# Second half of layer 0's last output projection, token-major, with the key/value stage re-cut by inner tiles

## The chip, the cores and the metric

The kernel runs on one core of a Trainium2 chip. The metric is device time in microseconds (us) for one execution, and the time of the kernel before is the median of three runs. A core has five engines that each run their own instructions strictly in the order in which they are issued: TensorE (PE in the profile; its weight loads are shown as PEld), VectorE (DVE), ScalarE (ACT), GpSimd (POOL) and SyncE (SP), which here issues nearly all DMAs. They wait for one another by semaphores.

## The reference, cut to what matters

A decoder trunk on 256 tokens of 1024 features, in float32. Layer 0 is FFN, short convolution, FFN; then one shared key/value projection is made from its output; layer 1 is FFN, sparse attention on that key/value, FFN. Around the change stand the second FFN of layer 0 and the projection `kv`:

```python
def rmsnorm(x, g):
    y = x * lax.rsqrt(jnp.mean(x * x, axis=-1, keepdims=True) + EPS)
    return y * g

def swiglu_ffn(x, w_in, w_out):              # w_in 1024 x 5632, w_out 2816 x 1024
    gate, up = jnp.split(x @ w_in, 2, axis=-1)
    return (jax.nn.silu(gate) * up) @ w_out

h = h + 0.5 * swiglu_ffn(rmsnorm(h, g), w_in, w_out)     # layer 0's second FFN
kv = (rmsnorm(h, kv_norm) @ w_kv)                        # w_kv 1024 x 1536
kv = kv.reshape(bsz, s, N_BRANCH, 2, N_KV_GROUPS, HEAD_DIM)
```

Branch 0 of `kv` (512 of its 1536 columns) goes on into a compression; branches 1 and 2 (the other 1024 columns: K of both, then V of both) are used as keys and values.

## The kernel before, in words

**Arithmetic.** Each float32 product is made of three matmuls. A weight is split into a high part `wh` and a low part `wl`, an activation into halves that lie side by side in one 128x512 tile (high for 256 tokens, low for 256 tokens), and high x high, low x high and high x low are summed in PSUM.

**Weights.** All weights come through one stream `W` in the order of their use. A chunk of 2048 columns (1 MB) is loaded by SyncE into one of three buffers `ws` (L139). Each chunk holds two units of 1024 columns; of each, ScalarE casts the high part (`wh`, L166) and VectorE subtracts to get the low part (`wl`, L183). There are six buffers of each. `take()` hands out the next unit; `done()` gives its buffer back and calls `pump()`, which issues the conversion of as many further units as have a free buffer. So where `done()` stands in the code is also where the next conversions stand in the queues of ScalarE and VectorE; and with the last unit of a chunk the load of the chunk two further on is issued to SyncE's queue. Nothing overtakes.

**The output projection** (`out_proj`, L471). The hidden activations are 22 tiles of 128 features (`act`). For the two FFN layers that end in it, the first 512 output features are made token-major: for each of the 22 tiles, six matmuls of 512 columns with the activation as the stationary operand (L492 to L494), 132 in all, into one pair of PSUM banks (`mm`). Two VectorE transposes of 32x32 blocks (L500) bring the result out; it goes to DRAM (`back`, two DMAs, L501) and comes back turned, features on the partitions (`come`, two DMAs, L507, into tiles `t`). `joined(m)` then adds two feature tiles to `h` (L513), makes the high halves of the two norms that follow (ScalarE, L294), the squares for the norm (ScalarE L309, summed on GpSimd L311), and the low halves (VectorE, L298). The last 512 features are made feature-major, in four tiles `c` = 4 to 7: for each, 22 matmuls of 512 columns (L532, the high weights) and 22 of 256 columns (L538, the low weights), then two adds from PSUM (L455) and the same norm steps. `joined(0)` and `joined(1)` are issued among these.

**The key/value stage.** Its inputs are `xkv[0..7]`, the normed tiles of `h`: 0 to 3 lie in `kt`, 4 to 7 in tiles `t`. K for all tokens runs over the eight `k`, 48 matmuls of 512 columns (L861 to L863), then V the same; then the four tiles of the compressed branch, eight matmuls of 512 (L351) and eight of 256 columns (L356) each. The sum of squares (`nm.halves()` on GpSimd, L317 and L318; `nm.rows()` on TensorE) becomes the factor `R` (ScalarE L329, VectorE L331), by which the results are scaled afterwards, not the inputs. So TensorE needs `xkv[k]` only when it gets to `k`, and `R` only for the outputs. After it comes the first FFN of layer 1 (L432 to L434).

Of the kernel before, what the change touches and what calls it, by code (L numbers as in the profile page):

```python
# [9 lines left out]
F32 = mybir.dt.float32  # L10
# [6 lines left out]
P = 128  # L17
# [51 lines left out]
def trunk(ctx, tc, A, out):  # L69
# [27 lines left out]
    def bank(shape=(P, 512)):  # L97
        return mk(shape, "a", 4, pool=ps)
# [186 lines left out]
    class Norm:  # L285
# [31 lines left out]
            po.tensor_copy(out=self.q[:, :T], in_=self.sq)  # L317
            po.tensor_tensor(out=self.q[:, T:], in0=self.sq, in1=self.q[:, :T].bitcast(F32), op=ALU.subtract)  # L318

        def rows(self):  # L320

            pb = bank()
            if self.q is None:
                pe.matmul(pb[:, :T], ones, self.sq, start=True, stop=True)
            else:
                for x in range(2):
                    pe.matmul(pb[:, :T], ones.bitcast(F32R), self.q[:, x * T:(x + 1) * T], start=(x == 0), stop=(x == 1))
            s = t1()
            ac.activation(s, pb[:, :T], AF.Sqrt, scale=1.0 / D, bias=epst)  # L329
            r = mk([P, T], "R", 2)  # L330
            ve.reciprocal(r, s)  # L331
            return r
# [135 lines left out]
        if c == ND - 1:  # L468
            norm.low(c)

    def out_proj(lhs, factor, norm, rest=None, cut=(7, 7, 7, 2)):  # L471

        n, i, u = len(lhs), 0, None
        if rest is None:
            head = [(bank(), W.take()[0]) for _ in range(4)]
            a_pass([(o, u, lhs, range(n)) for (o, u), n in zip(head, cut)])
            for c in range(4):
                o, u = head[c]
                a_pass([(o, u, lhs, range(cut[c], 8))])
                W.done(1, False)  # L480
                out_evac(o, c, factor, norm, True)
        else:
            n, o = NF, bank2()
            for k in range(NF):
                if k % 2 == 0:
                    u, = W.take()
                if k == 12:
                    rest()
                wh, wl = [u[x][:, (k % 2) * 512:(k % 2 + 1) * 512] for x in range(2)]
                for tt in range(2):  # L490
                    sh, sl = lhs[k][:, tt * P:(tt + 1) * P], lhs[k][:, T + tt * P:T + (tt + 1) * P]
                    pe.matmul(o[:, tt], sh, wh, start=(k == 0), stop=False)  # L492
                    pe.matmul(o[:, tt], sl, wh, start=False, stop=False)  # L493
                    pe.matmul(o[:, tt], sh, wl, start=False, stop=(k == NF - 1))  # L494
                if k % 2 == 1:
                    W.done()
            d = mk([2, 2, P, T], "back", 1, pool=dr)
            for tt in range(2):
                tb = mk([P, 768], "pr", 6)[:, :512]
                ve.transpose(tb, o[:, tt])  # L500
                sy.dma_start(d[:, tt].rearrange("m p n -> p m n"), tb.rearrange("p (m n) -> p m n", m=2))  # L501
            came = []

        def come():
            for m in range(2):
                came.append(t2([P, 2, T]))
                sy.dma_start(came[m].rearrange("p c (b j) -> p c b j", j=32),  # L507
                             d[m].rearrange("t (b i) (x c j) -> (i x) c (t b) j", i=32, c=2, j=32))

        def joined(m):  # L510
            cs = range(2 * m, 2 * m + 2)
            for c in cs:
                ve.scalar_tensor_tensor(out=h[c], in0=came[m][:, c % 2], scalar=factor, in1=h[c], op0=ALU.mult, op1=ALU.add)  # L513
            for c in cs:
                norm.high(c)
            for c in cs:
                norm.squares(c)
                norm.low(c)

        def tile():  # L520
            nonlocal i, u
            if i % 8 == 0:
                u, = W.take()
            q = slice(i % 8 * P, (i % 8 + 1) * P)
            i += 1
            return u[0][:, q], u[1][:, q], i % 8 == 0

        def wide(o, run, ks, last=None):
            for k in ks:
                while len(run) <= k:  # L530
                    run.append(tile())
                pe.matmul(o, run[k][0], lhs[k], start=(k == 0), stop=(k == last))  # L532

        def narrow(o, run, ks, last=None, free=True):
            for k in ks:
                while len(run) <= k:
                    run.append(tile())
                pe.matmul(o[:, :T], run[k][1], lhs[k][:, :T], start=False, stop=(k == last))  # L538
                if run[k][2] and free:
                    W.done(1, k < n - 1)  # L540

        c = 4
        while c < ND:
            o, run = bank(), []
            if n > 8 and c % 2 and c + 1 < ND:
                wide(o, run, range(n))
                o2, run2 = bank(), []
                wide(o2, run2, [0])
                joined(0)
                narrow(o, run, range(n), n - 1)  # L550
                out_evac(o, c, factor, norm)
                joined(1)
                narrow(o2, run2, range(n), free=False)
                wide(o2, run2, range(1, n), n - 1)
                for _ in range(sum(t[2] for t in run2)):
                    W.done(1, False)
                out_evac(o2, c + 1, factor, norm)
                W.pump(2)
                c += 2
                continue  # L560
            wide(o, run, range(n))
            narrow(o, run, range(n), n - 1)
            if n > 8 and c == 4:
                come()
            out_evac(o, c, factor, norm, n == 8)
            c += 1
        W.pump()
# [249 lines left out]
    def load_bias(j):  # L817
        pp, hg = divmod(j, 4)
        b = kt8[:, j, T:].rearrange("p (a n) -> p a n", a=2)
        src = bass.AP(tensor=row_d.tensor, offset=row_d.offset + (8 * pp + hg) * OHW,  # L820
                      ap=[[1, P], [4 * OHW, 2], [1, 256]])
        for a in range(2):
            if a == 0 or j < 4:
                sy.dma_start(b[:, a:] if j > 3 else b[:, a], src[:, a:] if j > 3 else src[:, a])
        bias[j] = b

    def c_bias(j):
# [15 lines left out]
    xk_a = mk([P, 4, 512], "kt", 1, F32R)  # L843
    xkv = [xk_a[:, k] for k in range(4)] + [t2(dt=F32R) for _ in range(4)]
    nm = Norm([(xkv, G_KV), (xs, G_FFN1 + 8)])
    out_proj(hid, 0.5, nm, rest=rest)
    nm.halves()
    del hid

    def b_full(xk, mid=None, shadow=None, o=None):  # L850
# [52 lines left out]

    kv = {}

    def kv_mid():
        kv["R"] = nm.rows()

    def kv_cols(k):

        if k != 1:
            return
        pt = bank2()[:, 0]
        for tt in range(2):
            pe.transpose(pt[:, tt * P:(tt + 1) * P], kv["R"][:, tt * P:(tt + 1) * P], ident)
        kv["rc"] = mk([P, 2], "rc", 2, pool=tiny)
        ve.tensor_copy(out=kv["rc"], in_=pt[:, 0:2 * P:P])
        kv["kns"] = scaled(ok, kv["rc"])

    ok = b_full(xkv, kv_mid)  # L920
    ov = b_full(xkv, None, kv_cols)
    rc, kns, R1 = kv["rc"], kv["kns"], kv["R"]
    for tt in range(2):
        ac.activation(V[tt], ov[tt], AF.Copy, scale=rc[:, tt:tt + 1])
    W.limit = 5

    own, other = [[act([P, 2, T], F32) for _ in range(2)] for _ in range(2)]
    for c in range(4):
        o, (u,) = bank(), W.take()
        a_pass([(o, u, xkv, range(8))])  # L930
        W.done()
        r = t1()
        ac.copy(r, o[:, T:])
        ve.tensor_tensor(out=r, in0=o[:, :T], in1=r, op=ALU.add)
        po.tensor_tensor(out=own[c // 2][:, c % 2], in0=r, in1=R1, op=ALU.mult)

    KT = mk([P, 2, 528], "kt", 1)
    raw = [mk([P, 16, 64], t, NBUF) for t in ("wh", "wl")]
# [508 lines left out]
def _layout(i):  # L1447
# [3 lines left out]
    for n in ("ffn1", "ffn2"):  # L1451
        w = a[n + "_w_in"]
        ins, outs = [], []
        for w, v, turn in zip(w.reshape(2, 1024, -1), a[n + "_w_out"], (0, n == "ffn2")):
            ins.append(w.reshape(8, 128, 2, NF // 2, 256).transpose(1, 3, 0, 2, 4).reshape(128, -1))
            v = v.reshape(-1, 4, 2, 32, 1024).transpose(0, 2, 3, 1, 4).reshape(-1, 1024)
            if turn:
                outs.append(v.reshape(NF, 128, 2, 512).transpose(1, 2, 0, 3).reshape(128, -1))
                continue
            first = v[:, :512].reshape(FF, 2, 2, 32, 4).transpose(0, 1, 4, 2, 3).reshape(NF, 128, 512).transpose(1, 0, 2)  # L1460
            v = v[:, 512:].reshape(NF, 128, 4, 128).transpose(1, 2, 0, 3)
            outs.append(np.concatenate([x.reshape(128, -1) for x in (first, v)], 1))
# [6 lines left out]
    r["conv_w_in"] = np.concatenate([cv, _rows(w[:, :1024])], 1)  # L1469
    r["conv_w_out"] = _rows(a["conv_w_out"][0])  # L1470
    w = a["w_kv"].reshape(8, 128, 3, 2, 256)
    parts = [p.reshape(8, 128, 512).transpose(1, 0, 2).reshape(128, -1) for p in (w[:, :, 1:, 0], w[:, :, 1:, 1])]
    r["w_kv"] = np.concatenate(parts + [_rows(w[:, :, 0].reshape(1024, 512))], 1)
    for n in ("cmp_w1_k", "cmp_w1_v"):
        r[n] = a[n].reshape(2, 16, 64, 128).transpose(0, 2, 1, 3).reshape(128, -1)
    w = a["attn_w_q"][0]
# [45 lines left out]
```

## Time and profile before

| | |
|---|---|
| runs of the kernel before | 949.6, 949.87, 949.9 us (median 949.87) |
| profiled execution, its own time | 949.64 us |
| span of its trace | 947.9 us (1.7 us lie outside it) |
| TensorE busy | 943.6 us, 4610 matmuls, granted clock 1.0 |
| VectorE, ScalarE, GpSimd busy | 653.8, 534.7, 111.8 us |
| read from and written to HBM | 190.80 and 16.29 MB |

How to read it: the profile's page gives busy time by engine, the chain of work that ended last, and the costliest groups of instructions. The timeline lists instructions in order with their start and length; `x22` means that 22 like instructions in a row were put in one row, and a bracket tells how long the engine idled before it and what released it. Matmuls are pipelined: a 512-column matmul is shown as 0.39 us long, while the next begins 0.227 us after it, so starts and not lengths are counted. The table of windows gives each engine's busy time, the granted TensorE clock and the DMA share of a stretch.

### The profile page before, as it was taken

The numbers are of one execution on the slowest core, as the hardware profiler recorded it, in microseconds if no ns is written. First come the engines' busy times: TensorE is split into PE (matmuls) and PEld (weight loads), VectorE is DVE, ScalarE is ACT, GpSimd is POOL, SyncE is SP. The second block draws the span as 40 slices with busy tenths as digits, with TensorE's granted clock in tenths as the row PEclk, the third lists the DMA queues.
The fourth block names the chain that finished last, engine by engine and source line by source line (L and its number), as shares of the span: only waits on it lengthen the run. The fifth ranks groups of instructions, "written<-read, shape, count | busy, mean of one in ns | idle before, by whom it ended". The sixth has DMA issues, their size and how long they took to land.

```text
span 947.9 us, 12791 instructions
## 1 busy us (share of the span) xinstructions
PE 943.6 (100%) x4610; PEld 789.1 (83%) x4610; DVE 653.8 (69%) x1066; ACT 534.7 (56%) x895; POOL 111.8 (12%) x191
## 2 busy tenths in 40 slices
PE   9999999999999999999999999999999999999998
PEld 8888888888888888888888888888877888888887
DVE  8767655778796667747757676856679787767552
ACT  7645543655465545545647775644589765445440
POOL 3000000211020000001121022200238120000000
PEclk9999999999999999999999999999999999999999
DMA  8888786658646998777647877776511248998750
GB/s 319 255 263 253 229 261 209 232 181 262 222 146 227 253 278 266 240 271 222 222 170 220 254 231 254 262 253 209 199 46 39 96 178 250 284 301 252 263 202 22
DMA packets 163966, 208.43 MB, mean 220 GB/s; under 512 B 124302, under 2 KB 140815, under 8 KB 143424
## 3 DMA queue, kind: packets, MB, share of 16 engines
q1 hardware_dynamic: 163758, 207.37, 67.2%
q8 instruction: 36, 0.59, 0.2%
q10 hardware_dynamic: 144, 0.26, 0.1%
q14 instruction: 28, 0.21, 0.1%
HBM read 190.80 MB, written 16.29 MB: 218 GB/s over the span
## 4 chain that ended last, share of the span: by engine, by line
PE 98%; DVE 1%; ACT 0%; issue 0%
PE mm L434 16%; PE mm L432 16%; PE mm L433 16%; PE a L532 7%; PE a L538 4%; PE mm L493 3%; PE mm L494 3%; PE mm L492 3%; PE a L351 3%; PE mm L655 2%; PE a L591 2%; PE a L590 2%; PE a L589 2%; PE a L356 2%; PE mm L723 2%; PE mm L725 2%
## 5 line engine op out<-in xcount | busy, mean ns | idle before, releaser
L183 DVE TENSOR_TENSOR wl<-ws,wh 128x1024 fp32r<-128x1024 f32 x316 | 387.0, 1245 | 214.0 <-ACT wh L166 205.3
L166 ACT CAST wh<-ws 128x1024 fp32r<-128x1024 f32 x316 | 326.4, 1051 | 230.1 <-DMA ws<-in_ffn_w_in_dram 98.1
L432 PE MATMUL mm<-wh,xs 128*128 128x512 f32 x656 | 255.9, 390 | 0.0
L434 PE MATMUL mm<-wl,xs 128*128 128x512 f32 x656 | 255.4, 389 | 0.0
L433 PE MATMUL mm<-wh,xs 128*128 128x512 f32 x656 | 255.3, 389 | 0.0
L434 PEld LDWEIGHTS mm<-wl,xs 128*128 128x128 f32 x656 | 123.1, 188 | 25.9 <-DVE wl L183 0.5
L433 PEld LDWEIGHTS mm<-wh,xs 128*128 128x128 f32 x656 | 123.2, 188 | 25.4
L432 PEld LDWEIGHTS mm<-wh,xs 128*128 128x128 f32 x656 | 123.2, 188 | 25.3
L311 POOL TENSOR_TENSOR sq<-sq,t 128x256 f32<-128x256 f32 x42 | 35.5, 846 | 385.9 <-ACT t L309 385.2
L390 ACT ACTIVATE t<-mm,rc 128x256 f32<-128x256 f32 x86 | 40.7, 474 | 59.1 <-DVE t L391 44.9
L532 PE MATMUL a<-act,wh 128*128 128x512 f32 x296 | 69.5, 390 | 0.0
L532 PEld LDWEIGHTS a<-act,wh 128*128 128x128 f32 x296 | 54.9, 188 | 11.0
L391 DVE SCALAR_TENSOR_TENSOR t<-mm,rc,t 128x256 f32<-128x256 f32 x86 | 41.5, 482 | 18.4 <-ACT t L390 15.1
L492 PE MATMUL mm<-wh,act 128*128 128x512 f32 x132 | 51.3, 389 | 0.0
L493 PE MATMUL mm<-wh,act 128*128 128x512 f32 x132 | 51.3, 389 | 0.0
L494 PE MATMUL mm<-wl,act 128*128 128x512 f32 x132 | 51.3, 389 | 0.0
L294 ACT ACTIVATE xs<-base 128x256 fp32r<-128x256 f32 x48 | 24.1, 507 | 44.9 <-DVE base L455 31.2
L359 ACT CAST act<-t 128x256 fp32r<-128x256 f32 x96 | 34.6, 405 | 13.0 <-DVE t L801 9.1
L392 DVE STREAM_TRANSPOSE t<-t 128x256 f32<-128x256 f32 x88 | 39.2, 446 | 3.1
L538 PEld LDWEIGHTS a<-act,wl 128*128 128x128 f32 x296 | 37.2, 191 | 1.0
L538 PE MATMUL a<-act,wl 128*128 128x256 f32 x296 | 37.5, 283 | 0.0
L360 DVE TENSOR_TENSOR act<-t,act 128x256 fp32r<-128x256 f32 x96 | 36.9, 423 | 0.5 <-ACT act L359 0.5
(278 smaller groups left out, 1196.5 us busy)
## 6 DMA issues: line engine op xcount, KB each, us to landing
ws<-in_ffn_w_in_dram SPq DMA_DIRECT2D x84, 1024.0 KB, 5.7
ws<-in_ffn_w_out_dram SPq DMA_DIRECT2D x44, 1024.0 KB, 5.6
turn<-t SPq DMA_DIRECT2D x48, 256.0 KB, 2.3
t<-turn SPq DMA_DIRECT2D x48, 256.0 KB, 7.0
ws<-in_conv_w_in_dram SPq DMA_DIRECT2D x12, 1024.0 KB, 5.1
ws<-in_w_kv_dram SPq DMA_DIRECT2D x6, 1024.0 KB, 5.2
ws<-in_conv_w_out_dram SPq DMA_DIRECT2D x4, 1024.0 KB, 5.4
ws<-in_attn_w_q_dram SPq DMA_DIRECT2D x4, 1024.0 KB, 5.5
```

Of the source, the lines that this page charges most:

```text
L166: ac.copy(h, src)
L183: ve.tensor_tensor(out=l, in0=src, in1=h.bitcast(F32), op=ALU.subtract)
L390: ac.activation(s, o[tt][:, :T], AF.Silu, scale=rc[:, tt:tt + 1])
L391: ve.scalar_tensor_tensor(out=s, in0=o[tt][:, T:], scalar=rc[:, tt:tt + 1], in1=s, op0=ALU.mult, op1=ALU.mult)
L432: pe.matmul(o[tt], sh, wh, start=(k == 0), stop=False)
L433: pe.matmul(o[tt], sl, wh, start=False, stop=False)
L434: pe.matmul(o[tt], sh, wl, start=False, stop=(k == 7))
L492: pe.matmul(o[:, tt], sh, wh, start=(k == 0), stop=False)
L493: pe.matmul(o[:, tt], sl, wh, start=False, stop=False)
L494: pe.matmul(o[:, tt], sh, wl, start=False, stop=(k == NF - 1))
L532: pe.matmul(o, run[k][0], lhs[k], start=(k == 0), stop=(k == last))
L538: pe.matmul(o[:, :T], run[k][1], lhs[k][:, :T], start=False, stop=(k == last))
```

## The change

For layer 0's second FFN alone, all 1024 features of the output projection are made token-major, in two halves of 132 matmuls each (`half`, called twice; the tile code above is not run there). The first half's result is fetched (`come`) at `k` = 6 of the second, and joined at `k` = 12 and 15. The second half's result goes to DRAM and comes back right after it, into buffers of `act`. It is joined (features 512 to 1023, which are `xkv[4..7]`) inside the key/value stage, by the `joined` that `out_proj` now returns.

The key/value stage is cut by inner tiles: `kv_full(k)` does K and V of one `k` (12 matmuls of 512 columns, one unit of weights). `kv_full(0..3)` come first, then `k` 0 to 3 of the compressed tiles `c0` and `c1`, then `joined(2)`, `kv_full(4)`, `joined(3)`, `kv_full(5)`, `k` 4 to 7 of `c0` and `c1`, the norm's rows, `kv_full(6)`, `kv_full(7)`, and tiles `c2`, `c3`. The weights lie in DRAM in that order: chunks [k0, k1], [k2, k3], [c0, c1], [k4, k5], [k6, k7], [c2, c3].

In all output projections with a token-major half, the last `done()` no longer pumps; `pump()` follows the half's transposes. `load_bias` issues one DMA where it issued two for four of its eight calls.

```diff
+        def half(step):
+            nonlocal u
+            o = bank2()
+            for k in range(NF):
+                if k % 2 == 0:
+                    u, = W.take()
+                step(k)
...
+                if k % 2 == 1:
+                    W.done(1, k < NF - 1)
+            d = mk([2, 2, P, T], "back", 1, pool=dr)
+            for tt in range(2):
+                tb = mk([P, 768], "pr", 6)[:, :512]
+                ve.transpose(tb, o[:, tt])
+                sy.dma_start(d[:, tt].rearrange("m p n -> p m n"), tb.rearrange("p (m n) -> p m n", m=2))
+            return d
...
+            n, d = NF, half(lambda k: rest() if k == 12 else None)
+            W.pump()
...
+        if whole:
+            d = half(lambda k: come() if k == 6 else joined(k // 3 - 4) if k in (12, 15) else None)
+            come(act)
+            W.pump()
+            return joined
...
-        for a in range(2):
-            if a == 0 or j < 4:
-                sy.dma_start(b[:, a:] if j > 3 else b[:, a], src[:, a:] if j > 3 else src[:, a])
+        for a in range(2):
+            if a == 0:
+                sy.dma_start(b, src)
...
-    out_proj(hid, 0.5, nm, rest=rest)
-    nm.halves()
+    joined = out_proj(hid, 0.5, nm, rest=rest, whole=True)
...
-    ok = b_full(xkv, kv_mid)
-    ov = b_full(xkv, None, kv_cols)
...
-    for c in range(4):
-        o, (u,) = bank(), W.take()
-        a_pass([(o, u, xkv, range(8))])
-        W.done()
...
+    def kv_full(k):
+        u, = W.take()
+        for x, o in enumerate((ok, ov)):
+            wh, wl = [w[:, x * 512:(x + 1) * 512] for w in u]
...
+    for k in range(4):
+        kv_full(k)
+        W.done()
+    co = bank2()
+    co, us = [bank(), co[:, 0], co[:, 1]], W.take(2)
+    a_pass([(o, u, xkv, range(4)) for o, u in zip(co, us)])
+    joined(2)
+    kv_full(4)
+    joined(3)
+    kv_full(5)
+    nm.halves()
+    a_pass([(o, u, xkv, range(4, 8)) for o, u in zip(co, us)])
+    W.done(4)
+    del us
+    pb = bank()
+    kv["R"] = nm.rows(pb)
+    for c in range(2):
+        cmp_sum(c, co[c])
+    kv_full(6)
+    W.done()
+    kv_full(7)
+    W.done()
+    kv_cols()
```

What this does to the queues is seen at two places.

VectorE before, from the last `joined` to the first conversions of the key/value stage. `wl_759` to `wl_770` are low halves of the first five units of `w_kv`, `t2_698` and `t2_699` are `xkv[6]` and `xkv[7]`, and `a_743`, `a_763` are the PSUM results of tiles 6 and 7:

```order
L298 SCALAR_TENSOR_TENSOR xs_690_3552<-base_79,xs_690_3552 128x256
L455 SCALAR_TENSOR_TENSOR base_79<-a_743_3852,base_79 128x256 x2
L298 SCALAR_TENSOR_TENSOR t2_698_3560<-base_79,t2_698_3560 128x256
L298 SCALAR_TENSOR_TENSOR xs_693_3555<-base_79,xs_693_3555 128x256
L183 TENSOR_TENSOR wl_759_3987<-ws_747_3874,wh_758_3985 128x1024
L183 TENSOR_TENSOR wl_762_3993<-ws_747_3874,wh_760_3989 128x1024
L183 TENSOR_TENSOR wl_765_4026<-ws_752_3900,wh_764_4024 128x1024
L183 TENSOR_TENSOR wl_768_4032<-ws_752_3900,wh_766_4028 128x1024
L183 TENSOR_TENSOR wl_770_4044<-ws_761_3991,wh_769_4042 128x1024
L455 SCALAR_TENSOR_TENSOR base_79<-a_763_3995,base_79 128x256 x2
L298 SCALAR_TENSOR_TENSOR t2_699_3561<-base_79,t2_699_3561 128x256
```

VectorE after, at the same place. `wl_764` and `wl_772` belong to tiles `c0` and `c1`, `wl_782` and `wl_785` to `k4` and `k5`, `wl_787` and `wl_790` to `k6` and `k7`; `mm_734` is the second half's result, `act_768` what came back of it, `t2_696` is `xkv[4]`, and L520 is the add of `joined(2)`:

```order
L183 TENSOR_TENSOR wl_764_3962<-ws_754_3894,wh_763_3960 128x1024
L493 STREAM_TRANSPOSE pr_766_3977<-mm_734_3759 128x512
L493 STREAM_TRANSPOSE pr_767_3980<-mm_734_3759 128x512
L183 TENSOR_TENSOR wl_772_3991<-ws_754_3894,wh_770_3987 128x1024
L183 TENSOR_TENSOR wl_782_4017<-ws_761_3944,wh_781_4015 128x1024
L183 TENSOR_TENSOR wl_785_4035<-ws_761_3944,wh_783_4031 128x1024
L183 TENSOR_TENSOR wl_787_4051<-ws_771_3989,wh_786_4049 128x1024
L183 TENSOR_TENSOR wl_790_4069<-ws_771_3989,wh_788_4065 128x1024
L520 SCALAR_TENSOR_TENSOR base_79<-act_768_3983,base_79 128x256 x2
L298 SCALAR_TENSOR_TENSOR t2_696_3554<-base_79,t2_696_3554 128x256
```

The add that makes `xkv[4]` now stands behind all conversions up to `k7`, whose chunk is `ws_771`; before, the adds of `xkv[4..6]` stood ahead of every conversion of `w_kv` shown here. ScalarE's queue has the same order: the casts of `k6` and `k7`, then the high half of `xkv[4]`.

SyncE before, from the transposed half's way out to the second chunk of `w_kv` (`ws_736` is the projection's last chunk, `ws_747` and `ws_752` the first two of `w_kv`):

```order
L501 DMA back_731_3756<-pr_732_3757 128x2x256
L501 DMA back_731_3756<-pr_733_3760 128x2x256
L139 DMA ws_736_3796<-in_ffn2_w_out_dram 128x2048
L507 DMA t2_740_3818<-back_731_3756 128x16x32
L507 DMA t2_741_3820<-back_731_3756 128x16x32
L139 DMA ws_747_3874<-in_w_kv_dram 128x2048
L139 DMA ws_752_3900<-in_w_kv_dram 128x2048
```

SyncE after, around the second half's way out and back (`ws_748`, `ws_754`, `ws_761`, `ws_771` and `ws_784` are the chunks [k2, k3], [c0, c1], [k4, k5], [k6, k7] and [c2, c3]; L494 and L513 are the DMAs that were L501 and L507):

```order
L139 DMA ws_748_3846<-in_w_kv_dram 128x2048
L139 DMA ws_754_3894<-in_w_kv_dram 128x2048
L139 DMA ws_761_3944<-in_w_kv_dram 128x2048
L494 DMA back_765_3976<-pr_766_3977 128x2x256
L494 DMA back_765_3976<-pr_767_3980 128x2x256
L513 DMA act_768_3983<-back_765_3976 128x16x32
L513 DMA act_769_3985<-back_765_3976 128x16x32
L139 DMA ws_771_3989<-in_w_kv_dram 128x2048
L139 DMA ws_784_4033<-in_w_kv_dram 128x2048
```

A second trip out and back is new, and the load of [k6, k7] stands behind it.

More of the change, by code (lines that the diff above doesn't have):

```diff
@@ L318, in halves, with rows @@
             po.tensor_tensor(out=self.q[:, T:], in0=self.sq, in1=self.q[:, :T].bitcast(F32), op=ALU.subtract)
-        def rows(self):
-            pb = bank()
+        def rows(self, pb=None):
+            pb = bank() if pb is None else pb
             if self.q is None:
@@ L469, in out_evac, with out_proj @@
             norm.low(c)
-    def out_proj(lhs, factor, norm, rest=None, cut=(7, 7, 7, 2)):
+    def out_proj(lhs, factor, norm, rest=None, cut=(7, 7, 7, 2), whole=False):
         n, i, u = len(lhs), 0, None
+        def half(step):
[5 more added lines that the diff above has]
+                step(k)
+                wh, wl = [u[x][:, (k % 2) * 512:(k % 2 + 1) * 512] for x in range(2)]
+                for tt in range(2):
+                    sh, sl = lhs[k][:, tt * P:(tt + 1) * P], lhs[k][:, T + tt * P:T + (tt + 1) * P]
+                    pe.matmul(o[:, tt], sh, wh, start=(k == 0), stop=False)
+                    pe.matmul(o[:, tt], sl, wh, start=False, stop=False)
+                    pe.matmul(o[:, tt], sh, wl, start=False, stop=(k == NF - 1))
+                if k % 2 == 1:
+                    W.done(1, k < NF - 1)
+            d = mk([2, 2, P, T], "back", 1, pool=dr)
+            for tt in range(2):
+                tb = mk([P, 768], "pr", 6)[:, :512]
+                ve.transpose(tb, o[:, tt])
+                sy.dma_start(d[:, tt].rearrange("m p n -> p m n"), tb.rearrange("p (m n) -> p m n", m=2))
+            return d
         if rest is None:
@@ L482, in out_proj, with come @@
         else:
[L483 to L495, printed above, removed]
-                    W.done()
[L497 to L501, printed above, removed]
+            n, d = NF, half(lambda k: rest() if k == 12 else None)
+            W.pump()
             came = []
-        def come():
+        def come(new=t2):
             for m in range(2):
-                came.append(t2([P, 2, T]))
+                came.append(new([P, 2, T], F32))
                 sy.dma_start(came[m].rearrange("p c (b j) -> p c b j", j=32),
@@ L511, in joined @@
             cs = range(2 * m, 2 * m + 2)
+            u = came.pop(0)
             for c in cs:
-                ve.scalar_tensor_tensor(out=h[c], in0=came[m][:, c % 2], scalar=factor, in1=h[c], op0=ALU.mult, op1=ALU.add)
+                ve.scalar_tensor_tensor(out=h[c], in0=u[:, c % 2], scalar=factor, in1=h[c], op0=ALU.mult, op1=ALU.add)
             for c in cs:
@@ L904, in trunk, with kv_cols, cmp_sum @@
     kv = {}
[L906 to L913, printed above, removed]
+    def kv_full(k):
+        u, = W.take()
+        for x, o in enumerate((ok, ov)):
+            wh, wl = [w[:, x * 512:(x + 1) * 512] for w in u]
+            for tt in range(2):
+                sh, sl = xkv[k][:, tt * P:(tt + 1) * P], xkv[k][:, T + tt * P:T + (tt + 1) * P]
+                pe.matmul(o[tt], sh, wh, start=(k == 0), stop=False)
+                pe.matmul(o[tt], sl, wh, start=False, stop=False)
+                pe.matmul(o[tt], sh, wl, start=False, stop=(k == 7))
+    def kv_cols():
         for tt in range(2):
-            pe.transpose(pt[:, tt * P:(tt + 1) * P], kv["R"][:, tt * P:(tt + 1) * P], ident)
+            pe.transpose(pb[:, T + tt * P:T + (tt + 1) * P], kv["R"][:, tt * P:(tt + 1) * P], ident)
         kv["rc"] = mk([P, 2], "rc", 2, pool=tiny)
-        ve.tensor_copy(out=kv["rc"], in_=pt[:, 0:2 * P:P])
-        kv["kns"] = scaled(ok, kv["rc"])
-    ok = b_full(xkv, kv_mid)
-    ov = b_full(xkv, None, kv_cols)
[L922 to L927, printed above, removed]
-    for c in range(4):
-        o, (u,) = bank(), W.take()
-        a_pass([(o, u, xkv, range(8))])
-        W.done()
+        ve.tensor_copy(out=kv["rc"], in_=pb[:, T::P])
+    def cmp_sum(c, o):
         r = t1()
@@ L934, in trunk @@
         ve.tensor_tensor(out=r, in0=o[:, :T], in1=r, op=ALU.add)
-        po.tensor_tensor(out=own[c // 2][:, c % 2], in0=r, in1=R1, op=ALU.mult)
+        po.tensor_tensor(out=own[c // 2][:, c % 2], in0=r, in1=kv["R"], op=ALU.mult)
+    own, other = [[act([P, 2, T], F32) for _ in range(2)] for _ in range(2)]
+    ok = bank2()
+    ok, ov = [ok[:, tt] for tt in range(2)], [bank(), bank()]
+    for k in range(4):
[21 more added lines that the diff above has]
+    kv_cols()
+    rc, R1 = kv["rc"], kv["R"]
+    for tt in range(2):
+        ac.activation(V[tt], ov[tt], AF.Copy, scale=rc[:, tt:tt + 1])
+    kns = scaled(ok, rc)
+    W.limit = 5
+    for c in (2, 3):
+        o, (u,) = co[2] if c == 2 else bank(), W.take()
+        a_pass([(o, u, xkv, range(8))])
+        W.done()
+        cmp_sum(c, o)
+    del co, pb
     KT = mk([P, 2, 528], "kt", 1)
@@ L1453, in _layout @@
         ins, outs = [], []
-        for w, v, turn in zip(w.reshape(2, 1024, -1), a[n + "_w_out"], (0, n == "ffn2")):
+        for w, v, turn in zip(w.reshape(2, 1024, -1), a[n + "_w_out"], ((0, 0), (2, 1))[n == "ffn2"]):
             ins.append(w.reshape(8, 128, 2, NF // 2, 256).transpose(1, 3, 0, 2, 4).reshape(128, -1))
             v = v.reshape(-1, 4, 2, 32, 1024).transpose(0, 2, 3, 1, 4).reshape(-1, 1024)
+            if turn == 2:
+                v = v.reshape(NF, 128, 2, 2, 2, 32, 4).transpose(1, 2, 0, 3, 6, 4, 5)
+                outs.append(v.reshape(128, -1))
+                continue
             if turn:
@@ L1471, in _layout @@
     w = a["w_kv"].reshape(8, 128, 3, 2, 256)
-    parts = [p.reshape(8, 128, 512).transpose(1, 0, 2).reshape(128, -1) for p in (w[:, :, 1:, 0], w[:, :, 1:, 1])]
-    r["w_kv"] = np.concatenate(parts + [_rows(w[:, :, 0].reshape(1024, 512))], 1)
+    full = w[:, :, 1:].transpose(1, 0, 3, 2, 4).reshape(128, 2, -1)
+    tiles = _rows(w[:, :, 0].reshape(1024, 512)).reshape(128, 2, -1)
+    r["w_kv"] = np.concatenate([full, tiles], 2).reshape(128, -1)
     for n in ("cmp_w1_k", "cmp_w1_v"):
```

## The prediction

> **What bounds the kernel now.** I read the page first, then TensorE's waits. On the page, the busy times and the chain that ended last:
>
> ```profile
> span 947.9 us, 12791 instructions
> PE 943.6 (100%) x4610; PEld 789.1 (83%) x4610; DVE 653.8 (69%) x1066; ACT 534.7 (56%) x895; POOL 111.8 (12%) x191
> PE 98%; DVE 1%; ACT 0%; issue 0%
> ```
>
> And all that TensorE waits for:
>
> ```profile
> PE a L250 <- PEq L1511: 0.8, 1, 0.8
> PE a L1273 <- ACT xs L1283: 0.4, 1, 0.4
> ```
>
> TensorE is the bound from end to end, so an edit can gain only by taking TensorE time away, and loses by making TensorE wait. The rest is read where the change sits, from TensorE's timeline (start, length):
>
> ```profile
> 394.81 0.39 PE L492 MATMUL mm<-wh,act 128*128 128x512 f32 x1
> ...
> 424.51 0.39 PE L494 MATMUL mm<-wl,act 128*128 128x512 f32 x1
> 424.73 5.15 PE L532 MATMUL a<-act,wh 128*128 128x512 f32 x22
> ...
> 452.64 2.79 PE L538 MATMUL a<-act,wl 128*128 128x256 f32 x22
> 455.27 0.40 PE L861 MATMUL a<-wh,kt 128*128 128x512 f32 x1
> ...
> 477.59 1.07 PE L351 MATMUL a<-kt,wh 128*128 128x512 f32 x4
> ...
> 479.41 0.64 PE L356 MATMUL a<-kt,wl 128*128 128x256 f32 x4
> 479.88 0.64 PE L356 MATMUL a<-t,wl 128*128 128x256 f32 x4
> ```
>
> One matmul starts right behind the other. A 512-column one takes (424.51 - 394.81)/131 = 0.2267 us, a 256-column one (455.27 - 452.64)/22 = 0.1196 us.
>
> **Part 1: matmuls.** The tile half took 455.27 - 424.73 = 30.54 us. Its replacement is 132 matmuls of 512 columns: 132 x 0.2267 = 29.92 us. Gain 0.6 us, certain. The key/value stage keeps its matmuls in number and size (96 of 512 columns for K and V, and 32 + 32 for the tiles) in another order: nothing. The adds from PSUM (L455) that go, the two new transposes, and the single bias DMA lie on engines that TensorE doesn't wait for; what decides is where the join stands.
>
> **Part 2: how long TensorE is covered.** Let T0 be the end of the second token-major half, 424.73 + 29.92 = 454.65 on the old clock. Before it needs `xkv[4]`, TensorE has `kv_full(0..3)`, 48 x 0.2267 = 10.88 us, and `c0`, `c1` over four `k`, 8 x 0.2267 + 8 x 0.1196 = 2.77 us. So `xkv[4]` must be ready by T0 + 13.65. In the old order the same tiles were joined before the stage began.
>
> **Part 3: when it is ready.** `joined(2)` stands on VectorE and ScalarE behind the conversions of `k6` and `k7`; their chunk stands on SyncE behind the second half's way out and back. So the chain is: transposes, out, back, chunk, two casts, two subtractions, join. Its pieces, on SyncE (issue times) and VectorE in the first half's trip:
>
> ```profile
> 425.80 1.23 DVE L183 TENSOR_TENSOR wl<-ws,wh 128x1024 fp32r<-128x1024 f32 x1 [1.50 <-ACT wh L166]
> 426.94 1.31 DVE L500 STREAM_TRANSPOSE pr<-mm 128x512 f32<-128x512 f32 x2
> ...
> 427.68 0.97 SPq L501 DMA_DIRECT2D back<-pr  x2
> 428.74 0.46 SPq L139 DMA_DIRECT2D ws<-in_ffn_w_out_dram  x1
> 430.62 3.23 SPq L507 DMA_DIRECT2D t<-back  x2
> ...
> 433.95 1.08 SPq L139 DMA_DIRECT2D ws<-in_w_kv_dram  x1
> ...
> DMA to landing us min/median/max: 6.9/6.9/6.9
> ```
>
> The last row is the landing of the chunk issued at 433.95: 6.9 us later, at 440.85. That trip had a 1 MB load (428.74) ahead of the way back. In the new order no load stands between out and back, so a nearer row for the second leg is a turn of the FFN stage, which went back in alone and had a chunk behind it:
>
> ```profile
> 400.49 0.59 SPq L399 DMA_DIRECT2D t<-turn  x1
> 401.18 1.24 SPq L139 DMA_DIRECT2D ws<-in_ffn_w_out_dram  x1
> L139 SPq DMA_DIRECT2D ws<-in_ffn_w_out_dram x1: 1243/1243/1243, 401.2 to 401.2; - x1
> DMA to landing us min/median/max: 6.3/6.3/6.3
> ```
>
> And the table of windows, whose last three columns are the granted clock, the DMA share and GB/s:
>
> ```profile
> 455.00:477.00 22.00, 22.00 (x102) 18.23 (x101) 15.52 (x16) 12.35 (x15) 4.02 (x5) 1.00 0.67 244
> ```
>
> From the issue of the turn's return to the landing of the chunk behind it: 401.18 + 6.3 - 400.49 = 6.96 us. Here two returns of the same 256 KB go ahead of the chunk, and the second adds 1.1 us (an estimate, 262 KB at the window's 244 GB/s). So 8.1 us.
>
> The start: the last half's result is out of the array at T0 + 0.2. The transposes also stand behind `c0`'s subtraction. That could end before T0, or, as in the quoted trip, 2.2 us after the half's last matmul (426.94 - 424.73), there behind one subtraction more. I take T0 + 0.9, the middle. From there by the rows the first return is issued 430.62 - 426.94 = 3.7 us later, T0 + 4.6; chunk landed 8.1 after it, L = T0 + 12.7.
>
> Bounds of L. Late: the old trip's own time from transposes to chunk, 440.85 - 426.94 = 13.9, from T0 + 0.9: T0 + 14.8. Early: transposes at T0 + 0.2, chunk issued 5.0 us later as the issues alone take, and landing in 4.5 us, as one that has the queues to itself does:
>
> ```profile
> L139 SPq DMA_DIRECT2D ws<-in_ffn_w_out_dram x1: 328/328/328, 418.9 to 418.9; - x1
> ...
> DMA to landing us min/median/max: 4.5/4.5/4.5
> ```
>
> That is T0 + 9.7. From L to TensorE's start, by these rows of ScalarE and VectorE:
>
> ```profile
> 438.17 2.94 ACT L166 CAST wh<-ws 128x1024 fp32r<-128x1024 f32 x3
> 439.24 3.71 DVE L183 TENSOR_TENSOR wl<-ws,wh 128x1024 fp32r<-128x1024 f32 x3 [1.07 <-ACT wh L166]
> ...
> 435.48 0.76 DVE L513 SCALAR_TENSOR_TENSOR base<-t,base 128x256 f32<-128x256 f32 x2
> 435.94 0.51 ACT L294 ACTIVATE kt<-base 128x256 fp32r<-128x256 f32 x1 [0.58 <-DVE base L513]
> 436.48 0.49 DVE L298 SCALAR_TENSOR_TENSOR kt<-base,kt 128x256 fp32r<-128x256 f32 x1 [0.24 <-ACT kt L294]
> ```
>
> The first subtraction begins 1.07 after the first cast; two take 3.71 x 2/3 = 2.4, so the join begins at L + 3.5. The high half is ready 436.45 - 435.48 = 0.97 later, the low half at 1.49; TensorE begins on the high one, and its second matmul, 0.23 later, waits 0.3 for the low one. The wait is L + 3.5 + 0.97 + 0.3 - (T0 + 13.65), that is L - T0 - 8.9. With L at 12.7: **3.8 us**. With the late L: 5.9.
>
> The early L does not bring it to nothing, because of the buffers. `k7`'s conversion is the sixth after `kv_full(3)`'s, whose buffer it needs, free at T0 + 10.88. Cast 1.05, subtraction 1.23, join 0.97 and 0.3: T0 + 14.4, a wait of 0.8 however early the chunk is. This floor decides for L under T0 + 9.7.
>
> What waits behind it: with `joined(2)` late, `joined(3)` follows 2.7 us later (435.48 to 438.17 for the old join), and TensorE has `kv_full(4)` and `kv_full(5)`, 24 x 0.2267 = 5.4 us, ahead of its need: covered by 2 us. The norm's rows follow on these rows of GpSimd and VectorE:
>
> ```profile
> 459.00 0.74 POOL L311 TENSOR_TENSOR sq<-sq,t 128x256 f32<-128x256 f32 x1 [8.05 <-ACT t L309]
> 459.80 0.40 POOL L317 CAST act<-sq 128x256 fp32r<-128x256 f32 x1
> 460.28 1.60 POOL L318 TENSOR_TENSOR act<-sq,act 128x256 fp32r<-128x256 f32 x1
> 466.35 1.75 DVE L331 RECIPROCAL R<-t 128x256 f32<-128x256 f32 x1 [0.56 <-ACT t L329]
> ```
>
> Last join to halves: 0.74 + 0.40 + 1.60 on GpSimd, and TensorE still has the tiles' second halves (2.77) behind its own need of `xkv[7]`: no wait, a margin below 1 us. `R` then has `kv_full(6)` and `(7)`, 5.4 us, as cover: none.
>
> Sum: -0.6 + 3.8 = +3.2 us. On the profiled execution 949.64 + 3.2 = 952.8; the median of the runs is 0.23 above it, so **953.1 us**.
>
> Does a wait of this size also slow TensorE's clock? The window quoted above shows a clock of 1.00, but no wait here is longer than 0.8 us, so the trace can't say what 3.8 us do; I take nothing. The Trainium skill (TensorE: Matmul & The Clock Gate, Part 1) says that a free-running window of about 3.4 us without work halves the clock until as long a busy window has passed. By that rule a gap of 3.5 us seldom holds a whole window, and the sum stays; a gap over 5 us would hold one about every second time and cost 1.7 us more, by that page an estimate.
>
> **The rivals.**
>
> A: as worked out, a wait of 2.5 to 5 us, 951.8 to 954.3. Chance 0.65.
>
> B, the other side: the chunk is early and the time is not slower. It decides at a wait of 2.5 us, L = T0 + 11.4: 1.3 us earlier than I take. For it: transposes at T0 + 0.2 take 0.7 off, and the lone load's 4.5 us against 6.3 show what an empty queue gives. Against: the returns are themselves in that queue. With the floor of 0.8 the time is 949.87 - 0.6 + 0.8 = 950.1; B spans 950.1 to 951.8. Chance 0.18.
>
> C: the join is ready within the cover altogether. It gives 949.3, the 0.6 us gained. For it speaks only that in the old trace no join made TensorE wait; against it the order of both queues. Chance 0.05.
>
> D: a longer wait, and a slow clock behind it. For it speaks the old trip's L. The slow rate shows in the trace only at the start:
>
> ```profile
> 0.77 3.75 PE L250 MATMUL a<-const-float32-1.0 128*128 128x128 f32 x16 [0.77 <-PEq L1511]
> 4.30 2.71 PE L655 MATMUL mm<-wh,xs 128*128 128x256 f32 x10
> 6.84 1.07 PE L655 MATMUL mm<-wl,xs 128*128 128x512 f32 x4
> ```
>
> There a 256-column matmul takes (6.84 - 4.30)/10 = 0.25 us, twice the later 0.12, for at most the 6.07 us from 0.77 to 6.84, of which half, 3.0, is lost. A wait of 5 us and a loss between 1.5 and 3.0 give 949.87 - 0.6 + 5 + 1.5 to 3.0 = 955.8 to 957.3. Chance 0.12.
>
> **How the numbers follow.** 0.2% is 1.9 us, about what a measurement of this kernel can tell from no change. Slower by more than that: A and D, 0.77. Faster by more needs 1.9 us where the rows show 0.6: 0.03 of C's share, for a cost in the old tile half that no record shows. The same: the rest of C and B, 0.20. The range reaches from just above B's floor, 950.3, to the edge of D, 955.5; C and the tops of D are left out.
>
> **What would show it.** Right: in TensorE's waits a line at the first matmul of `kv_full(4)`, 3 to 4.5 us, released by ScalarE's high half, with a short one for VectorE at the matmul behind it; ahead of it on VectorE the two subtractions of `k6`, `k7`, released by a chunk that lands 12 to 13.5 us after the second half's last matmul; 132 more matmuls of 0.2267 in place of the tiles. Wrong: no wait there, or under 1.5 us (B, and the chunk's landing time says why); a wait elsewhere, at the norm's rows or at `c2`'s weights, of more than 0.5 us; a clock below 1.00 in the windows behind the wait (D); or a wait whose last releaser is the way back itself, not the chunk behind it.

## The result, and the profile after

The changed kernel takes 955.49 us (median of 6 runs, 954.29 to 956.71), the kernel before 949.79 (6 runs, 949.54 to 950.21): a ratio of 1.006, 95% interval 1.0047 to 1.0073. The forecast was 953.1 within 950.3 to 955.5. The direction and the place are as forecast; the size is 2.4 us over the sum, which leaves the time 0.01 us inside the range. Most of the difference is one term, the clock of TensorE.

The profiled execution took 954.92 us. From its page, the span and the busy times:

```profile
span 953.1 us, 12699 instructions
PE 945.2 (99%) x4566; PEld 788.2 (83%) x4566; DVE 651.7 (68%) x1064; ACT 532.8 (56%) x895; POOL 112.0 (12%) x191
```

All that TensorE waits for (in total, times, longest):

```profile
PE mm L924 <- ACT t L294: 3.6, 1, 3.6
PE a L250 <- PEq L1557: 0.8, 1, 0.8
PE a L1314 <- ACT xs L1324: 0.4, 1, 0.4
```

There is one new line, 3.6 us at the first matmul of `kv_full(4)` (L924), released by ScalarE's high half of `xkv[4]`. TensorE has 44 matmuls fewer and yet 1.6 us more busy time. TensorE's timeline around the wait says why; the starts are to be read:

```profile
395.10 0.39 PE L485 MATMUL mm<-wh,act 128*128 128x512 f32 x1
...
454.94 0.39 PE L924 MATMUL mm<-wh,kt 128*128 128x512 f32 x1
...
468.11 0.64 PE L356 MATMUL mm<-kt,wl 128*128 128x256 f32 x4
472.35 0.50 PE L924 MATMUL mm<-wh,t 128*128 128x512 f32 x1 [3.61 <-ACT t L294]
472.87 0.50 PE L925 MATMUL mm<-wh,t 128*128 128x512 f32 x1
473.21 0.39 PE L926 MATMUL mm<-wl,t 128*128 128x512 f32 x1
473.43 0.53 PE L924 MATMUL mm<-wh,t 128*128 128x512 f32 x1
473.76 0.63 PE L925 MATMUL mm<-wh,t 128*128 128x512 f32 x1
474.19 0.63 PE L926 MATMUL mm<-wl,t 128*128 128x512 f32 x1
...
477.07 0.39 PE L924 MATMUL mm<-wh,t 128*128 128x512 f32 x1
```

The two token-major halves take 454.94 - 395.10 = 59.84 us, 264 x 0.2267; before, the half and the tiles took 455.27 - 394.81 = 60.46. `kv_full(4)` would have begun at 454.94 + 13.65 = 468.59 and begins at 472.35: 3.76 us. The first three matmuls take 473.43 - 472.35 = 1.08 instead of 0.68. The second waits for the low half, which VectorE has ready at 472.82 (0.29), and the third begins another 0.11 late, for a reason that the trace doesn't show: together 0.40. The next nine take 477.07 - 473.43 = 3.64 instead of 2.04: 1.60 us, with starts 0.43 apart where 0.227 is usual. The table of windows gives the granted clock (third column from the right), 1.00 for the first three matmuls and 0.52 for the rest:

```profile
472.50:473.40 0.90, 0.88 (x3) 0.52 (x4) 0.90 (x3) 0.90 (x3) 0.00 (x0) 1.00 0.70 137
473.40:476.80 3.40, 3.40 (x10) 2.62 (x9) 3.40 (x7) 2.58 (x8) 1.52 (x2) 0.52 0.62 258
```

So a slow clock of 3.4 us followed the wait. The sum: -0.6 for the matmuls, +3.76 + 0.40 + 1.60 = +5.2 us. The spans differ by 953.1 - 947.9 = 5.2 us.

What TensorE waited for, from the timelines of VectorE, SyncE and ScalarE; the first of the two loads at 461.56 is the chunk [k6, k7]:

```profile
456.08 1.30 DVE L493 STREAM_TRANSPOSE pr<-mm 128x512 f32<-128x512 f32 x2
...
459.65 1.81 SPq L513 DMA_DIRECT2D act<-back  x2
461.56 2.10 SPq L139 DMA_DIRECT2D ws<-in_w_kv_dram  x2
...
467.98 1.99 ACT L166 CAST wh<-ws 128x1024 fp32r<-128x1024 f32 x2 [6.52 <-DMA ws<-in_w_kv_dram]
469.06 2.36 DVE L183 TENSOR_TENSOR wl<-ws,wh 128x1024 fp32r<-128x1024 f32 x2 [6.34 <-ACT wh L166]
471.34 0.75 DVE L520 SCALAR_TENSOR_TENSOR base<-act,base 128x256 f32<-128x256 f32 x2
471.79 0.51 ACT L294 ACTIVATE t<-base 128x256 fp32r<-128x256 f32 x1 [1.82 <-DVE base L520]
472.33 0.49 DVE L298 SCALAR_TENSOR_TENSOR t<-base,t 128x256 fp32r<-128x256 f32 x1 [0.24 <-ACT t L294]
```

And that chunk's time from issue to landing:

```profile
DMA to landing us min/median/max: 6.3/6.3/6.3
```

ScalarE idles 6.5 us for the chunk and VectorE 6.3 us behind it, while the join stands behind these conversions on both, with its own data already there (the first experiment shows when).

### The profile page after: what moved, and what is told of

It reads as the page before. It is cut to its first block, busy times and chain, and to the rows that moved or that the text cites. A ratio compares the mean times of both kernels' runs of the same rounds, so it can differ in the third digit from the quotient of the medians.

```text
span 953.1 us, 12699 instructions
## 1 busy us (share of the span) xinstructions
PE 945.2 (99%) x4566; PEld 788.2 (83%) x4566; DVE 651.7 (68%) x1064; ACT 532.8 (56%) x895; POOL 112.0 (12%) x191
## 4 chain that ended last, share of the span: by engine, by line
PE 98%; DMA 1%; ACT 0%; DVE 0%; issue 0%; SPq 0%; ACTq 0%
PE mm L434 16%; PE mm L432 16%; PE mm L433 16%; PE a L539 5%; PE mm L486 4%; PE mm L487 4%; PE mm L485 4%; PE a L351 3%; PE a L545 3%; PE mm L668 2%; PE a L603 2%; PE a L602 2%; PE a L604 2%; PE a L356 2%; PE mm L736 2%; PE mm L737 2%
## 5 line engine op out<-in xcount | busy, mean ns | idle before, releaser
L485 PE MATMUL mm<-wh,act 128*128 128x512 f32 x176 | 68.5, 389 | 0.0
L486 PE MATMUL mm<-wh,act 128*128 128x512 f32 x176 | 68.5, 389 | 0.0
L487 PE MATMUL mm<-wl,act 128*128 128x512 f32 x176 | 68.5, 389 | 0.0
L539 PE MATMUL a<-act,wh 128*128 128x512 f32 x208 | 49.0, 390 | 0.0
L539 PEld LDWEIGHTS a<-act,wh 128*128 128x128 f32 x208 | 38.6, 188 | 7.7
L485 PEld LDWEIGHTS mm<-wh,act 128*128 128x128 f32 x176 | 33.0, 188 | 6.9
L486 PEld LDWEIGHTS mm<-wh,act 128*128 128x128 f32 x176 | 33.0, 188 | 6.8
L487 PEld LDWEIGHTS mm<-wl,act 128*128 128x128 f32 x176 | 33.0, 188 | 6.8
```

## The experiments

The explanation to be tested: the join waits in the queues of VectorE and ScalarE behind the conversions of `k6` and `k7`, and these wait for a chunk that stands on SyncE behind the second half's trip; the idle TensorE then loses clock. The rivals: the way back itself is too late; the new order of the stage costs by itself; the slow matmuls come of what else runs just then. The kernel before ran 21 times beside the first four kernels and 21 times beside the other four, with medians of 949.79 and 950.0 us.

**The joins ahead of the conversions.**

```diff
     for k in range(4):
         kv_full(k)
-        W.done()
+        W.done(1, k < 2)
...
     joined(3)
+    W.pump()
     kv_full(5)
```

> The two joins of the key/value stage stand ahead of the conversions of k6 and k7 on VectorE and ScalarE; nothing else is changed. If the wait comes from the queue order (the join behind conversions whose chunk is late), the join needs only what came back, which in the changed kernel landed 7.9 us after the second half's end, against 13.65 us of cover: no wait at kv_full(4), no slow clock, and the time is that of before less the 0.6 us of the matmuls, 949.2 us. If the way back itself is too long, or the new order of the stage costs by itself, a wait stays and the time is 952 us or more.

949.21 us (11 runs, 948.85 to 949.62), ratio 0.9993 (0.9985 to 1.0002). TensorE's waits in this kernel:

```profile
PE a L250 <- PEq L1558: 0.8, 1, 0.8
PE a L1315 <- ACT xs L1325: 0.4, 1, 0.4
PE mm L668 <- ACT xs L294: 0.2, 1, 0.2
```

And the join on VectorE's timeline:

```profile
463.45 0.76 DVE L520 SCALAR_TENSOR_TENSOR base<-act,base 128x256 f32<-128x256 f32 x2 [0.36 <-DMA act<-back]
```

No wait is left in the stage (L668 is the program's start). The join begins at 463.45, when its own data are there, 8 us ahead of where the changed kernel had it. The load of the chunk is issued where it was, behind the way back (461.92), and lands 7.3 us later, so that only the order on VectorE and ScalarE has changed. The way back was in time all along, and the new order of the stage costs nothing that these runs can tell.

**The chunk ahead of the trip.**

```diff
-        def half(step):
+        def half(step, last=False):
...
+            if last:
+                W.load(W.loaded)
             d = mk([2, 2, P, T], "back", 1, pool=dr)
...
-            d = half(lambda k: come() if k == 6 else joined(k // 3 - 4) if k in (12, 15) else None)
+            d = half(lambda k: come() if k == 6 else joined(k // 3 - 4) if k in (12, 15) else None, True)
```

> The chunk of k6 and k7 is loaded ahead of the second half's way out instead of behind its way back; the join stays behind the conversions. If the wait comes from the chunk, only the floor set by the six weight buffers is left: a wait of 0.8 to 1.1 us at kv_full(4), no slow clock, 950.1 to 950.4 us. If it comes from the join's own data or from the conversions as such, the wait stays near 3.6 us and the time near 955.5.

950.96 us (11 runs, 950.39 to 951.38), ratio 1.0011 (1.0002 to 1.002). TensorE's waits, without those at the start of the program and in later stages:

```profile
...
PE a L327 <- POOL act L318: 0.6, 1, 0.6
...
PE mm L926 <- ACT t L294: 0.3, 1, 0.3
```

From the timelines, the join on VectorE, `kv_full(4)` on TensorE, VectorE's subtractions behind the joins, GpSimd's part of the norm, and the norm's rows on TensorE:

```profile
466.81 1.23 DVE L183 TENSOR_TENSOR wl<-ws,wh 128x1024 fp32r<-128x1024 f32 x1 [1.50 <-ACT wh L166]
467.95 0.76 DVE L522 SCALAR_TENSOR_TENSOR base<-act,base 128x256 f32<-128x256 f32 x2
468.97 0.50 PE L926 MATMUL mm<-wh,t 128*128 128x512 f32 x1 [0.29 <-ACT t L294]
469.49 0.50 PE L927 MATMUL mm<-wh,t 128*128 128x512 f32 x1
...
474.93 4.55 DVE L183 TENSOR_TENSOR wl<-ws,wh 128x1024 fp32r<-128x1024 f32 x3 [0.95 <-ACT wh L166]
...
473.79 1.61 POOL L311 TENSOR_TENSOR sq<-sq,t 128x256 f32<-128x256 f32 x2 [1.68 <-ACT t L309]
475.46 1.27 POOL L317 CAST act<-sq 128x256 fp32r<-128x256 f32 x1
476.82 1.58 POOL L318 TENSOR_TENSOR act<-sq,act 128x256 fp32r<-128x256 f32 x1
...
477.58 0.28 PE L327 MATMUL a<-act,ones 128*128 128x256 f32 x1
478.45 0.39 PE L327 MATMUL a<-act,ones 128*128 128x256 f32 x1 [0.59 <-POOL act L318]
```

The 3.6 us are gone with the chunk's delay alone. What is left at `kv_full(4)` is the floor of the six buffers: `k7`'s subtraction (466.81) ends just ahead of the join, the wait is 0.3, and the second matmul begins 0.52 behind the first instead of 0.23. The time is still 0.6 us above the upper end of what was expected, 950.4. Most of that is a wait that was forecast as covered, 0.6 us at the norm's rows (L327): two adds, a cast and a subtraction on GpSimd end only at 478.40. It holds the second matmul there back by 0.75 us (478.45 instead of 477.58 + 0.12).

**TensorE kept busy in the wait.**

```diff
     joined(2)
+    for _ in range(14):
+        pe.matmul(co[2], us[0][0][:, :P], xkv[0], start=True, stop=True)
     kv_full(4)
```

> TensorE does 14 useless matmuls of 512 columns (3.2 us, into a bank that tile c2 overwrites later) in the wait before kv_full(4), which is otherwise as it was. If the slow matmuls behind the wait come from the clock dropping in an idle TensorE, they go, and the wait itself stays: 955.5 less 1.6 to 2.0, that is 953.5 to 953.9. If they are slow because of what else runs then (the joins on VectorE and ScalarE, the DMAs), the time stays 955.5.

954.89 us (5 runs, 954.08 to 955.35), ratio 1.0051 (1.0038 to 1.0064). TensorE's waits:

```profile
PE mm L924 <- ACT t L294: 1.1, 1, 1.1
...
PE a L327 <- POOL act L318: 0.6, 1, 0.6
```

And its timeline behind the wait:

```profile
473.07 0.50 PE L924 MATMUL mm<-wh,t 128*128 128x512 f32 x1 [1.08 <-ACT t L294]
...
474.17 0.39 PE L924 MATMUL mm<-wh,t 128*128 128x512 f32 x1
474.40 0.39 PE L925 MATMUL mm<-wh,t 128*128 128x512 f32 x1
```

The slow matmuls are gone (0.23 apart, granted clock 1.0 in all five runs) though the same joins and DMAs run beside them. So they came of the idle time. The trace and the clock show this; the times alone would not, since they overlap with those of the changed kernel. The time fell by 0.6 us and not by the 1.6 to 2.0 expected, for two reasons that the profile shows: the wait at the norm's rows appears, 0.7 us there, and the chunk landed 7.0 instead of 6.3 us after its issue in the profiled execution, so that `kv_full(4)` began 0.7 us later. Net of the first, the slow clock costs about 1.60 - 0.7 = 0.9 us. Why the landing varies stays open.

**Less of it filled: 5 and 9 matmuls** (the same edit with another number).

> As the run with 14 useless matmuls, but with 5 (1.1 us), so that TensorE idles 2.5 us instead of 3.6. If the clock drops only after a stretch of about 3.4 us without work, as the Trainium skill has it, it doesn't drop here: 953.5 to 953.9. If a shorter stretch does it too, slow matmuls stay and the time is 955 to 955.5.

954.94 us (5 runs, 953.94 to 955.45), ratio 1.0052 (1.004 to 1.0065).

> As the runs with 14 and 5 useless matmuls, with 9 (2.0 us): TensorE idles 1.6 to 2.4 us. With 1.1 us idle the clock dropped in none of 5 runs, with 2.8 in 3 of 5, with 3.6 in 6 of 6. If the drop depends on how an idle stretch lies in a free-running window and any mostly idle window does it, it comes here in fewer runs than at 2.8 us, 0 to 2 of 5, and the others lie near 954.2; if 2.8 was the threshold itself, in none.

954.79 us (5 runs, 954.38 to 955.24), ratio 1.0048 (1.0035 to 1.006). TensorE's wait at `kv_full(4)`, with 5:

```profile
PE mm L924 <- ACT t L294: 2.8, 1, 2.8
```

Its timeline behind that, with 5:

```profile
473.96 0.63 PE L924 MATMUL mm<-wh,t 128*128 128x512 f32 x1
474.39 0.63 PE L925 MATMUL mm<-wh,t 128*128 128x512 f32 x1
```

And the wait with 9:

```profile
PE mm L924 <- ACT t L294: 1.9, 1, 1.9
```

An idle stretch of 2.8 us was enough for the slow clock in the profiled execution. Each run lists its mean clock; 3.4 us at half clock take 0.002 off the mean of 953 us, so a run with a drop has 0.998 or less. The idle stretch is known for the profiled execution alone; the other runs of a kernel may differ from it by some tenths, as the landing of the chunk does:

| kernel | idle stretch in its profile, us | runs with the drop |
|---|---|---|
| 14 matmuls | 1.1 | 0 of 5 |
| 9 matmuls | 1.9 | 2 of 5 (954.79, 955.10; without: 954.38, 954.76, 955.24) |
| 5 matmuls | 2.8 | 3 of 5 (954.94, 955.21, 955.45; without: 953.94, 954.54) |
| the change | 3.6 | 6 of 6 |
| one more MB (below) | 8.3 | 4 of 4 |

The longer TensorE idles, the more often the drop came in these few runs. That a stretch of about 3.4 us is needed did not hold: with 5 matmuls the drop and the 2.8 us are in the same execution. With 9 matmuls the profiled execution (954.38) had none, so the 1.9 us are not those of a run with the drop. With 5 matmuls the runs with the drop average 955.20 us and the others 954.24, about the 0.9 us above; with 9 matmuls the times overlap.

**One more megabyte ahead of the chunk.**

```diff
             come(act)
+            sy.dma_start(mk([P, CHUNK], "extra", 1, pool=dr), W.src[0])
             W.pump()
```

> One more 1 MB transfer (from one place in DRAM to another, read by nobody) stands on SyncE between the second half's way back and the chunk of k6 and k7. If that chunk is what the join waits for, the wait at kv_full(4) grows by what the transfer takes, 3 to 4.5 us, to 6.5 to 8, the clock drops as before, and the time is 958.5 to 960.5. If the join waits for its own data, it stays 955.5.

959.6 us (4 runs, 958.44 to 959.83), ratio 1.0095 (1.0081 to 1.0109). TensorE's wait:

```profile
PE mm L925 <- ACT t L294: 8.3, 1, 8.3
```

The cast of `k6` on ScalarE's timeline, which waits for the chunk:

```profile
472.72 1.99 ACT L166 CAST wh<-ws 128x1024 fp32r<-128x1024 f32 x2 [11.23 <-DMA ws<-in_w_kv_dram]
```

And the window behind the wait, with its clock of 0.50:

```profile
477.00:480.40 3.40, 3.31 (x8) 2.50 (x9) 3.33 (x6) 2.58 (x8) 1.52 (x2) 0.50 0.92 308
```

The cast begins 472.72 - 467.98 = 4.7 us later and the wait is 8.3 - 3.6 = 4.7 us longer: one for one. The forecast for the wait was 6.5 to 8.

**The side edits alone,** on the kernel before.

```diff
-                    W.done()
+                    W.done(1, k < NF - 1)
...
+            W.pump()
             came = []
...
-            if a == 0 or j < 4:
-                sy.dma_start(b[:, a:] if j > 3 else b[:, a], src[:, a:] if j > 3 else src[:, a])
+            if a == 0:
+                sy.dma_start(b, src)
```

> The kernel before with only the two side edits: one bias DMA instead of two in four calls, and the pump of a token-major half's last unit behind its transposes. Every theory here has these at nothing: 949.8 us, TensorE's waits as before. If they cost or gain, it shows here by over 0.5 us.

950.06 us (11 runs, 949.57 to 950.88) against 950.0, ratio 1.0 (0.9991 to 1.0009). Nothing, as expected.

**Both mends.** The edits of the first two experiments together.

> Both mends: the joins ahead of the conversions of k6 and k7, and their chunk loaded ahead of the way out. If the queue order alone is the cause, the second mend adds nothing to the first: 949.2 us, no wait at kv_full(4). If the return is slowed by the load that now goes ahead of it, the join comes some 2 us later, still within the cover: the same 949.2.

949.04 us (11 runs, 948.82 to 950.24), ratio 0.9991 (0.9982 to 0.9999). The join on VectorE:

```profile
464.72 0.76 DVE L522 SCALAR_TENSOR_TENSOR base<-act,base 128x256 f32<-128x256 f32 x2 [2.44 <-DMA act<-back]
```

The load ahead makes the way back 1.3 us later (464.72 against 463.45), within the cover. The second mend adds nothing that these runs can tell from the first alone. This version and the one with the first mend lie below both kernels, by 0.96 and 0.58 us against the kernel before, near the 0.6 of the matmuls; only the interval of this one lies wholly below 1.

## Why the prediction came out as it did

- **Matmuls, -0.6 us: right.** 59.84 us for two halves where 60.46 stood, and 949.21 and 949.04 against 949.79 and 950.0 once the wait is gone.
- **Cover, 13.65 us: right** to the row (468.59).
- **The chain: right in each link.** With T0 at 454.94 the transposes began at T0 + 1.1 (taken: 0.9), the first return was issued at T0 + 4.7 (4.6), the chunk landed 8.2 us after it (8.1), at T0 + 12.9 (12.7). The wait, 3.76 + 0.40 = 4.16 us, was forecast as 3.8. Moving the join took it away, moving the chunk left 0.3 of the 3.6 us of idling, and delaying the chunk lengthened it one for one: shown. (401.18 + 6.3 - 400.49 is 6.99 and not 6.96, which leaves the 8.1 as it is.)
- **The clock, "I take nothing": wrong.** This term of the sum measured 1.60 us in the profiled execution, and it is the main one that put the time 2.4 us off. The forecast asked for an idle stretch over about 3.4 us, or 5 for an even chance, and put the drop into rival D at 0.12 with a wait of 5 us. It came with 3.6 us in six of six runs, and in a profiled execution with 2.8. D's mechanism was at work beside A's, at A's wait, and a clock below 1.00 behind the wait was one of the forecast's own signs of being wrong. The 1.60 lie in D's bounds, 1.5 to 3.0; net of the next term they are 0.9.
- **The norm's rows, "no wait, a margin below 1 us": wrong by its margin.** GpSimd takes 1.61 + 1.27 + 1.58 us as the rows of the second experiment give them, where 0.74 + 0.40 + 1.60 were summed: two adds stand in `joined`, and the cast took longer. The wait of 0.6 us shows only where TensorE runs at full clock after a late join. In the changed kernel GpSimd ended 1.6 us ahead of the norm's rows on TensorE:

```profile
478.30 1.55 DVE L183 TENSOR_TENSOR wl<-ws,wh 128x1024 fp32r<-128x1024 f32 x1 [0.95 <-ACT wh L166]
480.91 1.23 DVE L183 TENSOR_TENSOR wl<-ws,wh 128x1024 fp32r<-128x1024 f32 x1 [1.06 <-ACT wh L166]
...
480.18 0.74 POOL L318 TENSOR_TENSOR act<-sq,act 128x256 fp32r<-128x256 f32 x1
...
482.56 0.40 PE L327 MATMUL a<-act,ones 128*128 128x256 f32 x2
```

  The slow clock had held TensorE back by 1.60 us, and GpSimd's last step was shorter. It took 0.74 us in the three profiles in which no subtraction was running on VectorE when it began (the change, 5 matmuls, one more MB), and 1.58 to 1.60 in the seven in which one was. That the subtraction causes the difference was not tested.
- **The side edits at nothing: right.**
- **The range: luck.** 955.49 lies between the top of A, 954.3, and the foot of D, 955.8, where no rival was; it is inside the range by 0.01 us because the range was drawn up to D. The forecast was right in the cause and the place of the wait, not in the whole of the cost.
- The rest: the profiled execution came to 954.92 where the sum gave 952.8; of these 2.1 us 1.60 is the clock and 0.36 the wait. The median lies 0.6 above it, which is the spread of the runs. The slowest (956.71) has a mean clock of 0.996, twice the loss of the others; where its second drop lies is open.

## What to carry to other kernels

An instruction that the critical engine needs must not be issued behind work that serves a later need: here an edit of two lines that lets two conversions wait for the joins is worth 6 us (955.49 to 949.21). When a step is moved, follow each queue that it now stands in, and ask whether anything ahead of it there waits for a transfer that the step doesn't need. A wait of TensorE can cost more than its length: here the clock halved behind 3.6 us in every run and behind 2.8 us in three of five, so a wait of this size is priced with the slow clock behind it. Part of that price may be hidden by a wait that the delay covers further on, here 0.7 of 1.6 us.

## What the runs showed of the hardware that was not expected

TensorE's clock dropped to half for 3.4 us (0.52 granted over 473.40 to 476.80) behind idle stretches, not all of them as long as that: in 2 of 5 runs of a kernel with 1.9 us in its profile, 3 of 5 with 2.8, 6 of 6 with 3.6, and in none of 5 with 1.1. The drop need not be there when the work resumes: after 3.6 us of idling the first three matmuls still had a clock of 1.00; after 8.3 us it was 0.50 from the first. The Trainium skill (TensorE: Matmul & The Clock Gate, Part 1) has the window free-running and 3.4 us long, with which the length of the slow stretch agrees, and that the drop comes in some runs and not in others. That a whole window must be idle does not agree with the drop behind 2.8 us in one profiled execution, nor with six of six at 3.6, a gap that would by that rule seldom hold a whole window. What share of a window is enough stays open.
